# A two-layer mixing, memory and feed-forward block: the queues of four engines ordered by a timeline model

## The chip, the cores and the metric

The kernel runs on one core of a Trainium2 chip. The time is device time in microseconds (us) of one execution; lower is better. The engines are TensorE (PE; PEld is its weight load), VectorE (DVE), ScalarE (ACT), GpSimd (POOL) and SyncE (SP), which issues most loads. Each engine takes its own instructions in order, and waits on semaphores for the others.

## The reference

One sequence of 256 tokens with 2048 columns goes through two layers. Each layer has a mixing step (an RWKV-7 recurrence with 16 heads of 64 beside causal attention with 8 heads on low-rank queries and keys), a cross attention to 256 memory rows, and a feed-forward step of width 8192 with a squared ReLU.

```python
for l in range(DEPTH):
    u = rms_norm(h, mix_pre_g[l])
    proj = u @ w_in[l]                      # layer 1: with w_in_vres beside it
    y_rwkv, v_first = rwkv7_time_mix(proj[..., :RWKV_IN], ...)
    y_mla = mla_heads(proj[..., RWKV_IN:IN_WIDTH], ...)
    y = concatenate([y_rwkv, y_mla]) @ w_out[l]
    h = h + rms_norm(y, mix_post_g[l])
    u = rms_norm(h, mem_pre_g[l])
    h = h + rms_norm(memory_cross_attention(u, mem_n, ...), mem_post_g[l])
    u = rms_norm(h, ffn_pre_g[l])
    y = square(relu(u @ w_ff1[l])) @ w_ff2[l]
    h = h + rms_norm(y, ffn_post_g[l])
```

## The kernel before, in words

Every weight matrix is read once, in units of 512 KB. `units` (L259 on) loads a unit into a buffer `raw` (five of them) from SP. `split` (L283) makes two parts of it: ACT casts `wh` from `raw` (L291), and DVE subtracts to give the rest `wl` (L292). `wh` and `wl` lie in a ring of four buffers, some units in longer-lived ones. The left-hand side has two parts too, and `go` issues three matmuls for each product (`mm`, L243):

```python
    def go(self, o, x, wh, wl, start, stop):
        xh, xl = x
        self.mm(o, xh, wh, start, False)
        self.mm(o, xh, wl, False, False)
        self.mm(o, xl, wh, False, stop)
```

Activations `h` are turned by PE transposes (L248) in blocks of 128 x 512 (`x`). `toT` makes `uf` from such a block on DVE (L397), its first part `uh` on ACT (L398), and the rest `ul` (L399), on DVE for block 0 and on POOL for blocks 1 to 3. `sumsq` (L375) squares `h` on ACT for the norm (tile `junk`); `finish` adds the normed result to `h` on DVE (L455, four rows for each half of the tokens).

In a mixing step the heads come in two groups. `f_group` builds for each group the tiles AR (L658, L663) and BK (L664, L666), products `prod` (L671), and from shifted columns `yp` (L466), `yd` (POOL, L471) the tile vT (L474). In layer 1 vT is mixed with the first layer's values: POOL works on `vf` (L813, L814), DVE adds it (L815). `f_inner` multiplies BK by AR on PE and masks the result to W on DVE (L693); ACT copies pieces to G (L695). `f_fs` then runs 31 steps on DVE, each of a product (L768) and a sum (L770) into T, which give the triangular inverse of a chunk; POOL and ACT copy it to Tb (L775, L776), DVE transposes that to Ud (L779) and Tr (L781), and PE uses Tr with W. Attention has its query copies `qn` on ACT (L1085) and its softmax in `f_lane` (rows L1115 to L1125, maximum `nm` on DVE, exponentials `pr` on ACT). The feed-forward step begins with `ff1_first` (L1320 relu `rf`, L1309 and L1310 its split), then goes on in eight blocks.

The order of PE's queue is written out by hand: fibres (Python generators) are spawned with due times in an estimated time `clk` and polled between matmuls, and this decides where the transposes and small matmuls stand. The scope `tc.manual_schedule(engines={mybir.EngineType.PE})` in `_build` (L1482 on) keeps PE's instructions in the order of the program. The queues of DVE, ACT, POOL and SP are ordered by the framework's own scheduler, from the same program. What it may move is bounded by the data and by buffers: a tile is written only when the readers of its buffer's former content are done.

## Time and profile before

| what | value |
|---|---|
| median of 3 runs (lowest to highest) | 2586.59 us (2586.35 to 2586.64) |
| the profiled execution's own time | 2588.6 us |
| its span, first to last instruction | 2586.8 us |
| mean granted clock of PE | 0.987 |
| PE busy | 2524.0 us (98%) |
| DVE, ACT, POOL busy | 1557.1, 1209.3, 444.6 us |
| data moved by DMA | 456.76 MB, mean 177 GB/s |

The span is what lies between the first and the last instruction of the profiled execution, and 1.8 us less than its own time. In a timeline row the first two numbers are start and duration in us; what stands in brackets at the end is the engine's idle time before the row and what ended it. Names are tiles without their buffer numbers: `g` and `x` are accumulators of PE. In the table of waits the three numbers are the sum, the count and the longest.

### The profile page before, as it was taken

The page shows a single profiled execution, that of the slowest core. Times are in us where ns is not written, and L with a number is a line of the kernel's source. Part 1 is how long each engine was busy: PE and PEld are TensorE (multiplying, and loading weights), DVE is VectorE, ACT ScalarE, POOL GpSimd, SP SyncE. Part 2 cuts the span into 40 slices and gives each one's busy share as a digit, 9 for nine tenths or more (in the row PEclk, how much of TensorE's full clock was granted, in tenths as well). Part 3 has the DMA queues.
Part 4 walks back from the last instruction along what each step waited for, and adds up shares of the span by engine and source line. Part 5 has one row for each costly group of instructions (what it writes and reads, how often), then busy time and mean ns, then how long its engine had stood idle before and what let it go on. Part 6 is the DMA issues. An engine that isn't in the chain of part 4 may idle for free.

```text
span 2586.8 us, 43201 instructions
## 1 busy us (share of the span) xinstructions
PE 2524.0 (98%) x17458; PEld 2285.7 (88%) x17458; DVE 1557.1 (60%) x2121; ACT 1209.3 (47%) x1724; POOL 444.6 (17%) x597
## 2 busy tenths in 40 slices
PE   8999999999999999999999998999999999999998
PEld 7989888989899889989788987889898998899896
DVE  4777966664454555555757778666644555545555
ACT  5454555554444344444454545545544444444443
POOL 3324425220000000000124245202200000000000
PEclk9999999999999999999999999999999999999999
DMA  6454446646656655666654544565456556556663
GB/s 228 151 158 136 132 158 216 216 131 184 191 187 187 188 189 186 188 192 204 199 168 135 158 117 132 168 214 187 136 182 189 187 181 194 190 186 188 192 204 131
DMA packets 257176, 456.76 MB, mean 177 GB/s; under 512 B 25588, under 2 KB 58740, under 8 KB 256976
## 3 DMA queue, kind: packets, MB, share of 16 engines
q1 hardware_dynamic: 247600, 422.79, 51.8%
q0 software_dynamic: 9376, 31.21, 3.8%
q8 instruction: 137, 2.24, 0.4%
q14 instruction: 63, 0.52, 0.1%
HBM read 444.50 MB, written 9.44 MB: 175 GB/s over the span
## 4 chain that ended last, share of the span: by engine, by line
PE 86%; DVE 6%; POOL 2%; issue 2%; DMA 1%; ACT 1%; SPq 0%; DVEq 0%; POOLq 0%; ACTq 0%
PE g L243 77%; PE x L243 7%; DVE wl L292 2%; PE x L248 2%; DVE fs L768 1%; DVE T L770 1%; DVE h L455 1%; DMA raw<-in_w_ff_dram 1%; ACT wh L291 1%; DMA vf<-vfirst 0%; DMA raw<-in_w_in_dram 0%; POOL yd L471 0%; POOL rsn L617 0%; POOL kT L837 0%; POOL vf L814 0%
## 5 line engine op out<-in xcount | busy, mean ns | idle before, releaser
L292 DVE TENSOR_TENSOR wl<-raw,wh 128x1024 fp32r<-128x1024 f32 (+2 forms) x804 | 978.1, 1222 | 736.9 <-ACT wh L291 733.3
L291 ACT CAST wh<-raw 128x1024 fp32r<-128x1024 f32 (+2 forms) x804 | 834.2, 1041 | 980.4 <-PE g L243 903.4
L243 PE MATMUL g<-uh,wh 128*128 128x256 f32 x2816 | 808.1, 287 | 0.0
L243 PE MATMUL g<-uh,wl 128*128 128x256 f32 x2816 | 797.9, 283 | 0.4 <-DVE wl L292 0.4
L243 PE MATMUL g<-ul,wh 128*128 128x256 f32 x2816 | 797.7, 283 | 0.0
L243 PEld LDWEIGHTS g<-uh,wh 128*128 128x128 f32 x2816 | 541.0, 192 | 5.3 <-issue 2.3
L243 PEld LDWEIGHTS g<-uh,wl 128*128 128x128 f32 x2816 | 541.3, 192 | 3.0 <-issue 1.7
L243 PEld LDWEIGHTS g<-ul,wh 128*128 128x128 f32 x2816 | 541.1, 192 | 0.0
L243 PE MATMUL g<-wl,hdh 128*128 128x512 f32 x1024 | 398.9, 390 | 0.4 <-DVE wl L292 0.4
L243 PE MATMUL g<-wh,hdh 128*128 128x512 f32 x1024 | 398.9, 390 | 0.0
L243 PE MATMUL g<-wh,hdl 128*128 128x512 f32 x1024 | 398.5, 389 | 0.0
L1349 POOL TENSOR_TENSOR rl<-rl 128x512 f32<-128x512 f32 x60 | 61.3, 1041 | 1171.6 <-ACT rl L1348 1171.5
L243 PEld LDWEIGHTS g<-wl,hdh 128*128 128x128 f32 x1024 | 192.3, 188 | 40.5 <-DVE wl L292 1.3
L243 PEld LDWEIGHTS g<-wh,hdl 128*128 128x128 f32 x1024 | 192.3, 188 | 39.9
L243 PEld LDWEIGHTS g<-wh,hdh 128*128 128x128 f32 x1024 | 192.3, 188 | 39.4
L243 PE MATMUL g<-wh,uh 128*128 128x256 f32 (+3 forms) x320 | 114.6, 358 | 12.2 <-ACT uh L398 7.9
L243 PE MATMUL g<-wl,uh 128*128 128x256 f32 (+3 forms) x320 | 109.8, 343 | 3.9 <-DVE wl L292 3.9
L243 PE MATMUL g<-wh,ul 128*128 128x256 f32 (+3 forms) x320 | 109.6, 343 | 1.6 <-POOL ul L399 1.1
L1352 DVE TENSOR_TENSOR hdl<-rl,hdh 128x512 fp32r<-128x512 f32 x60 | 47.6, 794 | 67.7 <-ACT hdh L1351 67.7
L1369 DVE SCALAR_TENSOR_TENSOR y<-g,s,y 128x512 f32<-128x512 f32 x112 | 79.0, 744 | 10.6 <-PE g L243 10.6
L243 PEld LDWEIGHTS g<-wh,uh 128*128 128x128 f32 x320 | 63.9, 200 | 19.3 <-ACT uh L398 9.7
L243 PEld LDWEIGHTS g<-wl,uh 128*128 128x128 f32 x320 | 63.9, 200 | 9.6 <-DVE wl L292 5.9
(341 smaller groups left out, 2991.8 us busy)
## 6 DMA issues: line engine op xcount, KB each, us to landing
raw<-in_w_ff_dram SPq DMA_DIRECT2D x512, 512.0 KB, 4.2
raw<-in_w_in_dram SPq DMA_DIRECT2D x112, 512.0 KB, 4.4
raw<-in_w_out_dram SPq DMA_DIRECT2D x64, 512.0 KB, 3.9
raw<-in_wk_mem_dram SPq DMA_DIRECT2D x16, 512.0 KB, 4.1
raw<-in_wq_mem_dram SPq DMA_DIRECT2D x16, 512.0 KB, 3.8
raw<-in_wv_mem_dram SPq DMA_DIRECT2D x16, 512.0 KB, 4.8
raw<-in_wo_mem_dram SPq DMA_DIRECT2D x16, 512.0 KB, 3.6
raw<-in_w_in_dram SPq DMA_DIRECT2D x16, 448.0 KB, 5.1
```

What stands on the lines that cost most here:

```text
L243: return self.nc.tensor.matmul(out, lhsT, rhs, start=start, stop=stop, skip_group_check=skip)
L248: self.nc.tensor.transpose(out, in_, self.ident[p0 : p0 + n, p0 : p0 + n])
L291: nc.scalar.copy(out=wh, in_=raw)
L292: nc.vector.tensor_tensor(out=wl, in0=raw, in1=wh.bitcast(F32), op=ALU.subtract)
L455: nc.vector.scalar_tensor_tensor(out=h[t][c], in0=y[t][c], scalar=rs, in1=h[t][c], op0=ALU.mult, op1=ALU.add)
L768: nc.vector.tensor_tensor(out=tmp, in0=N[:, s + 1 :, s : s + 1].to_broadcast([128, m, w]), in1=T[:, s : s + 1, :w].to_broadcast([128, m, w ...
L770: nc.vector.tensor_tensor(out=T[:, s + 1 :, :w], in0=T[:, s + 1 :, :w], in1=tmp, op=ALU.add)
L1349: nc.gpsimd.tensor_tensor(out=r, in0=r, in1=r, op=ALU.mult)
L1352: nc.vector.tensor_tensor(out=hl[:, 2 * q : 2 * q + 2, :], in0=r, in1=o.bitcast(F32), op=ALU.subtract)
L1369: nc.vector.scalar_tensor_tensor(out=o, in0=ps, scalar=s2[t], in1=o, op0=ALU.mult, op1=ALU.add)
```

## The change

One argument is given to the framework. Its scheduler then plans the order of the queues with its timeline model of the engines; before, it planned without that model.

```diff
-    with tile.TileContext(nc) as tc:
+    with tile.TileContext(nc, schedule_with_timeline_sim=True) as tc:
         _build(nc, tc, aps, out)
```

PE keeps its order, all 15368 rows. DVE has 2041 rows after 2042, and 1551 lines of difference; ACT 738 lines, POOL 240, SP 16, all of these near the program's start: three weight loads and the constants C (L534) now stand ahead of the last four loads of `h`. Nothing is computed in another way, and tiles and buffers are the same. Three places follow, as pieces of the difference: a minus is where a row stood before, a plus where it stands now. The number behind a name tells tiles of the same name apart.

The first piece is DVE's queue in layer 0, at the end of the second group (about 268 to 281 us of the profile before). BK_3021 is written there for the last time, vT_3264 is what PE transposes next, and the `wl` are weight subtractions.

```order
 L664 TENSOR_TENSOR BK_3021<-bb_3224,en_3219 128x4x64
+L466 TENSOR_TENSOR yp_3265<-g_2707,rbc_403 128x2x256
 L665 TENSOR_TENSOR kT_2692<-kT_2692,ka_3226 128x256
-L671 SCALAR_TENSOR_TENSOR prod_3256<-rT_2256,V,kT_2692 128x256
-L666 TENSOR_TENSOR BK_3021<-kT_2692,en_3219 128x4x64
+L466 TENSOR_TENSOR yp_3272<-g_2708,rbc_403 128x2x256
 L671 SCALAR_TENSOR_TENSOR prod_3258<-rT_2256,V,kT_2692 128x256
 L671 SCALAR_TENSOR_TENSOR prod_3260<-rT_2256,V,kT_2692 128x256
+L292 TENSOR_TENSOR wl_3514<-raw_3510,wh_3513 128x1024
+L666 TENSOR_TENSOR BK_3021<-kT_2692,en_3219 128x4x64
```

The last BK row now stands behind the `yp` rows, two more `prod` rows and a `wl`; two further `wl` have moved up, one ahead of this piece and one between the vT rows, all three from places behind the vT and W rows.

The second piece is DVE's queue in layer 1, in the second group (about 1570 to 1582 us). W_16327 is the last of four masked products; vT_16267 is summed with what POOL left in `vf`.

```order
 L693 TENSOR_TENSOR W_16306<-x_16308,C 128x512
-L815 TENSOR_TENSOR vT_16267<-vT_16267,vf_16342 128x512
-L815 TENSOR_TENSOR vT_16267<-vT_16267,vf_16347 128x512
+L292 TENSOR_TENSOR wl_16495<-raw_16491,wh_16494 128x1024
 L693 TENSOR_TENSOR W_16327<-x_16328,C 128x512
 L693 TENSOR_TENSOR W_16327<-x_16329,C 128x512
-L292 TENSOR_TENSOR wl_16495<-raw_16491,wh_16494 128x1024
+L815 TENSOR_TENSOR vT_16267<-vT_16267,vf_16342 128x512
 L700 STREAM_TRANSPOSE N_16358<-G_16224 64x1024
+L815 TENSOR_TENSOR vT_16267<-vT_16267,vf_16347 128x512
```

The two L815 rows, which wait for POOL, have moved behind W, and a `wl` has moved ahead of it.

The third place is the entry of the feed-forward part in layer 1 (about 1846 to 1873 us). On DVE, the rows `uf` of blocks 1 and 2 stand before as follows, and now:

```order
 L451 TENSOR_REDUCE pss_19211<-pp_18990 128x1
+L397 TENSOR_TENSOR uf_19226<-x_19221,V 128x512
+L397 TENSOR_TENSOR uf_19235<-x_19230,V 128x512
 L399 TENSOR_TENSOR ul_18979<-uf_19207,uh_18975 128x4x128
 L455 SCALAR_TENSOR_TENSOR h_16855<-y_18987,prs_19213,h_16855 128x512 x2
 L455 SCALAR_TENSOR_TENSOR h_16856<-y_18988,prs_19213,h_16856 128x512 x2
-L397 TENSOR_TENSOR uf_19226<-x_19221,V 128x512
-L397 TENSOR_TENSOR uf_19235<-x_19230,V 128x512
```

They have moved ahead of the `ul` of block 0 and of the four h rows. On ACT, some 15 us later, wh_19489 is the cast of the last weight unit that `ff1_first` uses for its second quarter:

```order
-L291 CAST wh_19471<-raw_19469 128x1024
 L375 ACTIVATE junk_19441,ss_19440<-h_16855 128x512
 L375 ACTIVATE junk_19443,ss_19440<-h_16855 128x512
 L375 ACTIVATE junk_19445,ss_19440<-h_16856 128x512
 L375 ACTIVATE junk_19447,ss_19440<-h_16856 128x512
-L291 CAST wh_19489<-raw_19487 128x1024
+L291 CAST wh_19471<-raw_19469 128x1024
 L291 CAST wh_19576<-raw_19574 128x1024
-L1320 ACTIVATE rf_19466<-g_19403 128x256
 L291 CAST wh_19582<-raw_19580 128x1024
 L291 CAST wh_19612<-raw_19610 128x1024
+L291 CAST wh_19489<-raw_19487 128x1024
```

The cast wh_19489 stands three casts later, and wh_19471 behind the four `junk` rows; above this piece one `uh` row has moved behind three more `junk` rows. Layer 0 has the same moves at its own entry. Inside the eight feed-forward blocks one `wh` cast has moved ahead of the first split of each half block, and its `wl` likewise.

## The prediction

> **What bounds the kernel now.** I read the page first: busy times, then the chain that ended last.
>
> ```profile
> PE 2524.0 (98%) x17458; PEld 2285.7 (88%) x17458; DVE 1557.1 (60%) x2121; ACT 1209.3 (47%) x1724; POOL 444.6 (17%) x597
> PE 86%; DVE 6%; POOL 2%; issue 2%; DMA 1%; ACT 1%; SPq 0%; DVEq 0%; POOLq 0%; ACTq 0%
> ```
>
> TensorE (PE) is busy for 2524.0 of 2586.8 us, and PE's own queue is the same row for row after the change. So the time can move in two ways only: PE waits more or less, or its matmuls run at another granted clock. Next I read the table of waits of PE, and then the two long feed-forward stretches and two stretches around a wait in the table of stretches (length, busy time of PE, PEld, DVE, ACT, POOL, granted clock, DMA share, GB/s).
>
> ```profile
> PE g L243 <- ACT uh L398: 7.9, 5, 2.0
> PE g L243 <- ACT qn L1085: 6.4, 2, 3.5
> PE x L248 <- DVE vT L474: 5.0, 5, 2.4
> PE g L243 <- DVE wl L292: 4.7, 8, 1.6
> PE g L243 <- ACT wh L291: 4.3, 2, 3.2
> PE x L248 <- DVE rsn L616: 2.1, 2, 1.5
> ...
> 594.00:1258.00 664.00, 664.00 (x4269) 608.46 (x4268) 346.07 (x321) 287.58 (x311) 32.79 (x34) 1.00 0.60 189
> 1884.00:2548.00 664.00, 664.00 (x4270) 608.51 (x4269) 346.02 (x321) 287.66 (x311) 32.78 (x34) 1.00 0.60 189
> ...
> 1846.00:1852.00 6.00, 3.40 (x16) 2.79 (x16) 5.26 (x10) 0.92 (x2) 1.22 (x2) 0.69 0.00 0
> 1852.00:1860.00 8.00, 7.08 (x37) 6.79 (x38) 4.89 (x7) 4.65 (x7) 3.74 (x3) 0.60 0.17 50
> ```
>
> The two feed-forward stretches, 1328 us together, have PE busy for all of their length at clock 1.00: no order of the other queues can gain there. The waits lie in short places of the mixing stages and at the entry of the feed-forward part. Each row has total, count and longest; no wait is longer than 4.3 us, so this is a list of small prices. 0.2% of this kernel is 5.2 us, about what a measurement can tell from no change.
>
> **The change part by part.** No instruction is added. I take the places where PE waits and follow the new queue order by hand, with durations from the rows.
>
> *Start, +1.5 (0 to +4).* SP now issues three weight loads and the constants ahead of the last four loads of `h`, and ACT does two sums of squares (`junk`) ahead of the first `uh` and the second weight cast.
>
> ```profile
> 6.58 3.42 SPq L1402 DMA_DIRECT2D h<-in_x_dram  x4
> 14.15 0.63 ACT L375 ACTIVATE junk<-h 128x512 f32<-128x512 f32 x1
> 13.63 0.74 PE L243 MATMUL g<-wl,uh 128*128 128x448 f32 x1 [1.00 <-DVE wl L292]
> ```
>
> PE already waits there for what follows that cast. Two steps of 0.63 us and their read-outs make 1.5 us; the upper end adds most of the 3.42 us that the four loads are put back.
>
> *State-forming chain of the first group in each layer, −2.6 (−2.6 to +2.3).* The subtractions `wl` (four of 1.22 us) now stand ahead of rows of the serial chain L768/L770. Of the 4.7 us in the `wl` row of the waits, four lie here, one of 1.55 and three of 0.29 to 0.40; these go. The chain's end moves 4 × 1.22 = 4.9 us later, and this is covered:
>
> ```profile
> 157.77 0.41 PE L243 MATMUL g<-wl,uh 128*128 128x320 f32 x1 [1.55 <-DVE wl L292]
> 167.49 0.17 DVE L770 TENSOR_TENSOR T<-T,fs 128x16 f32<-128x16 f32 x1
> 173.95 0.64 POOL L775 COPY Tb<-T 64x512 f32<-64x512 f32 x1
> ```
>
> The next reader of `T` is a copy on POOL, which runs 6.3 us after the chain's end, behind other rows. If that cover were gone, the 4.9 us would count against the 2.6.
>
> *Group steps: first and second group of layer 0, first of layer 1: +1.3 (−4 to +7).* In the second group three `wl` of 1.21 to 1.22 us pass the last BK and vT rows (order shown above).
>
> ```profile
> 269.99 0.41 DVE L666 TENSOR_TENSOR BK<-kT,en 128x256 f32<-128x256 f32 x1
> 275.69 1.21 DVE L292 TENSOR_TENSOR wl<-raw,wh 128x1024 fp32r<-128x1024 f32 x1
> 274.73 1.57 PE L248 MATMUL x<-Id,vT 128*128 128x128 f32 x4 [2.44 <-DVE vT L474]
> ...
> 120.82 0.30 PE L248 MATMUL x<-Id,vT 128*128 128x128 f32 x1 [1.13 <-DVE vT L474]
> 1408.94 1.31 PE L243 MATMUL x<-AR,BK 64*128 64x128 f32 x10 [0.94 <-DVE W L693]
> 1416.19 1.18 PE L243 MATMUL x<-AR,BK 64*128 64x128 f32 x4 [3.92 <-DVE W L693]
> ```
>
> The transposes of vT at 274.73 wait already, so two to three `wl` make them 2.4 to 3.6 us later. But the W rows that follow no longer have these `wl` ahead of them, and reach their old times within 8 us: I take +1.5. The group at 120.82 has the same move with a shorter wait (+1.0). In layer 1 the BK stands about 4 us later (+3.5 at 1403), while W passes one of two L815 rows, which removes most of 0.94 + 3.92 = 4.86: −1.2. Sum +1.3. The lower end keeps only the gains, the upper one only the losses.
>
> *Second group of layer 1, −2.0 (−5 to +2).* Two L815 rows waited for POOL and held W behind them; now `wl` and W stand ahead of both.
>
> ```profile
> 1573.56 1.75 DVE L815 TENSOR_TENSOR vT<-vT,vf 128x512 f32<-128x512 f32 x1 [2.02 <-POOL vf L814]
> 1577.09 1.28 DVE L693 TENSOR_TENSOR W<-x,C 128x512 f32<-128x512 f32 x2
> 1577.83 0.66 PE L248 MATMUL x<-Id,BK 128*128 128x128 f32 x4 [1.72 <-DVE W L693]
> 1582.98 0.39 PE L243 MATMUL g<-qTh,wh 128*128 128x256 f32 x1 [1.07 <-ACT qrx L1061]
> 1585.38 1.12 PE L248 MATMUL x<-Id,vT 128*128 128x128 f32 x4 [0.99 <-ACT tok L722]
> 1627.13 2.12 DVE L781 STREAM_TRANSPOSE Tr<-Tb 64x1024 f32<-64x1024 f32 x1
> 1629.62 1.56 PE L243 MATMUL x<-Tr,W 32*32 32x32 f32 x38
> ```
>
> DVE's idle time began at 1573.56 − 2.02 = 1571.5; W ends at 1571.5 + 1.22 + 1.28 = 1574.0 in place of 1578.4, and 1.72 + 1.07 + 0.99 = 3.8 us of waits go, with about 1 of the 3.5 us for `qn`. But Tr ended 0.37 us before PE wanted it at 1629.62, and the chain before it is all DVE work, with attention rows of about 3 us now put ahead. DVE gets back its idle 2.02 and a little more, less these 3. So most of the 4.8 us is taken back at Tr; I keep 2.0.
>
> *Query copies, layer 0: 0 (−1.4 to +1.5).* The copies `qn` no longer stand behind a softmax row that waits for DVE, which takes 1.4 us from the wait at 319.89; attention rows placed ahead of Tr move its end from 334.97 by 5 to 6 us, to about PE's need.
>
> ```profile
> 319.89 0.80 PE L243 MATMUL g<-wh,oh 128*128 128x512 f32 x1 [2.86 <-ACT qn L1085]
> 332.81 2.16 DVE L781 STREAM_TRANSPOSE Tr<-Tb 64x1024 f32<-64x1024 f32 x1
> 340.74 1.45 PE L243 MATMUL x<-Tr,W 32*32 32x32 f32 x40
> ```
>
> *Entry of the feed-forward part, both layers, −0.4 (−9 to +5).*
>
> ```profile
> 1848.32 2.74 DVE L455 SCALAR_TENSOR_TENSOR h<-y,prs,h 128x512 f32<-128x512 f32 x4 [0.71 <-POOL prs L255]
> 1850.98 1.88 DVE L397 TENSOR_TENSOR uf<-x,V 128x512 f32<-128x512 f32 x3
> 1852.37 0.58 PE L243 MATMUL g<-wh,uh 128*128 128x256 f32 x1 [1.81 <-ACT uh L398]
> 1853.72 0.58 PE L243 MATMUL g<-wh,ul 128*128 128x256 f32 x1 [0.55 <-POOL ul L399]
> 1869.14 1.03 ACT L291 CAST wh<-raw 128x1024 fp32r<-128x1024 f32 x1
> 1872.09 0.28 PE L243 MATMUL g<-wh,uh 128*128 128x256 f32 x1
> ```
>
> Two `uf` now stand ahead of `ul` and the four h rows. 1.81 + 0.55 = 2.4 us of wait go, and `ul` of the first block comes 1.2 us later, where PE waits: −1.2 a layer. Beside that there is the clock: PE's 7.08 busy us at 0.60 would take 4.25 at full clock, so up to 2.8 more; I take half. Against both stands the cast that ends at 1870.2, 1.9 us before PE needs it. It now has all eight `junk` steps and three other casts before it, and its `wl` ends about 2.5 us too late. So 2 × (−1.2 − 1.4 + 2.5) ≈ −0.2, and −0.4 with the slightly longer waits of layer 0.
>
> [...]
>
> *Entry of layer 1 and the group norm, −1.0 (−2 to 0).* In the rows for `wh` (longest 3.2) and `rsn` (2.1 in two) one row each moves ahead by about 0.5 us.
>
> Sum: +1.5 − 2.6 + 1.3 − 2.0 + 0 − 0.4 − 1.0 = −3.2 us. The profiled execution took 2588.6 us with a span of 2586.8, so it would take 2585.4; the median of the runs is 2.0 us lower, 2586.6, and gives **2583.4 us**.
>
> **The rivals.**
>
> A, the gains are kept: DVE has enough idle time that nothing given back is late. −2.6 − 3.8 − 1.4 − 1.0 − 2 × 1.2 − 2 × 1.4 − 1.0 − 0.5 (group steps) + 1.5 = −14.0: 2572.6. For it: DVE is busy for 60%. Against it: at 1627 the chain is DVE's, with 0.37 us to spare.
>
> B, slower: weight subtractions stand ahead of rows that PE waits for. A `wl` row needs its cast on ACT, and DVE stands still behind it. In three group steps the last BK comes 3.4 to 3.5 us late (about 4.8 of push less a margin of 1.4, as at 269.99 against PE's vT at 274.73), 10.2 in all, not regained by W; the casts in front of the feed-forward part cost 5.0 less 2.4; the start 1.5; kept are 2.6 and 2.0: +9.7, 2596.3. It decides as soon as the push of BK is above the margin of 1.4 us and the W rows do not catch up. For it: vT is already waited for in five places. Against it: the same `wl` work leaves later rows free.
>
> C, no effect: the queues differ, but PE's order is fixed and each loss meets a gain of its size: within 1 us, 2586.6. The two stretches without a wait speak for it, the 1577 place against it.
>
> **How the numbers follow.** My forecast 0.44, its own range −9 to +3 (2577.6 to 2589.6); A 0.25; B 0.22; C 0.09. The range takes in A and B with about 2 us beyond each: 2570 to 2598. Faster by over 0.2%: all of A and a third of the forecast, 0.40. Slower: B and a little of the forecast, 0.24. The rest, 0.36, is within 0.2%.
>
> **What would show it.** In the new profile the waits of PE for `wl` around 154 to 167 us should be gone, the `uh` row should fall from 7.9 to about 5, W before 1578 should have no wait, and waits for Tr near 1625 and for `wh` near 1872 should appear. The feed-forward stretches must stay at clock 1.00 with PE fully busy. Wrong would be a wait inside these stretches, a start longer by over 4 us, or PE waits that in sum change by more than 15 us.

## The result and the profile after

The changed kernel is slower: 2600.82 us in the median of four runs (2598.75 to 2602.91), against 2586.57 us (2586.35 to 2586.64) for the kernel before. The ratio is 1.0053, with a 95% interval of 1.004 to 1.0066: 14.2 us more. The forecast was 2583.4 us with a range up to 2598. The profiled execution took 2598.75 us, the lowest of the four, with a span of 2597.0 us and a mean granted clock of 0.988; against the profiled execution of before (span 2586.8) that is +10.2 us, and this is what the traces can account for. The other 4 us are 2.0 by which before's profiled execution lies above its median and 2.1 by which this one lies below its own. What is given below as measured is the median of fast runs, and one execution of 2749.43 us is left out as slow.

The page's busy times and chain of the changed kernel, to be held against the two lines that open the prediction:

```profile
PE 2524.7 (97%) x17458; PEld 2283.2 (88%) x17458; DVE 1576.4 (61%) x2121; ACT 1212.6 (47%) x1724; POOL 457.8 (18%) x597
PE 78%; DVE 7%; ACT 2%; issue 2%; POOL 1%; DMA 1%; DVEq 0%; POOLq 0%; ACTq 0%
```

PE's busy time is the same within 0.7 us, and the rows of the table of waits sum to 59.8 us after and to 49.7 before: over the whole program the 10.2 us appear as waiting. In single places it is otherwise, since the granted clock rose in some (1.00 in place of 0.69 and 0.60 at layer 1's entry) and fell in others (0.79 in place of 1.00 in layer 0's first group). The table of waits of PE, after (sum, count, longest):

```profile
PE g L243 <- DVE wl L292: 8.9, 8, 2.3
PE x L243 <- DVE BK L666: 8.3, 3, 4.1
PE g L243 <- ACT wh L291: 6.5, 5, 3.0
PE x L248 <- DVE vT L474: 5.0, 4, 2.2
...
PE x L248 <- DVE pr L1125: 3.7, 2, 2.4
PE g L243 <- DVE ul L399: 3.4, 4, 1.3
PE x L243 <- DVE ri L1122: 3.3, 1, 3.3
PE x L248 <- POOL qr L1000: 3.1, 1, 3.1
PE g L243 <- ACT uh L398: 2.8, 5, 0.7
```

The waits that the planner was to remove are gone or smaller: `uh` fell from 7.9 to 2.8, `qn` (6.4) and the 4.8 us for W have left the head of the table. In their place stand BK (8.3, no such row before), `pr`, `ri`, `qr`, more `wl` (4.7 before) and more `wh` (4.3 before). So waits were exchanged, at a loss.

Where this happens is seen by taking the same PE instruction in both traces (PE's queue is the same row for row) and subtracting its starts. The table gives how much this distance grew in each part of the program, worked out so from the traces, in us; the last four columns are experiments of the next section.

| part (where it ends in the profile before) | predicted | after | DVE alone planned | DVE alone held | gains only | entries only |
|---|---|---|---|---|---|---|
| start (45) | +1.5 | +3.0 | -0.1 | +1.1 | +0.2 | +0.3 |
| layer 0, first group (137) | +1.0 | +3.8 | +5.5 | +1.6 | 0.0 | 0.0 |
| state-forming chains, both layers | -2.6 | -3.7 | -3.7 | -1.3 | -3.7 | -0.2 |
| layer 0, second group (290) | +1.5 | +3.4 | +5.2 | +2.1 | +0.1 | +0.2 |
| layer 0, `qn` to Tr (345) | 0 | -0.6 | +1.0 | +0.1 | -1.1 | -1.4 |
| entries of the feed-forward part, both, front (556 to 569, 1846 to 1859) | -0.4 with the next row | -12.7 | -10.3 | +0.3 | -10.4 | -10.6 |
| the same, back (to 592, to 1885) | | +13.3 | +6.6 | +3.9 | +4.9 | +4.9 |
| feed-forward, 592 to 1250 and 1885 to 2540 | 0 | 0.0 | 0.0 | 0.0 | 0.0 | 0.0 |
| ends of the feed-forward part (1277, 2575) | not in the sum | +5.2 | -0.5 | +8.0 | +0.2 | +3.3 |
| entry of layer 1 and group norm (1320, 1548) | -1.0 | -2.7 | -2.7 | -1.9 | -3.6 | -1.1 |
| layer 1, first group (1424) | -1.2 | +0.2 | -1.8 | +0.1 | 0.0 | +0.2 |
| layer 1, second group to Tr (1640) | -2.0 | +1.1 | +4.9 | +2.2 | -3.4 | +1.5 |
| sum | -3.2 | +10.3 | +4.1 | +16.3 | -16.7 | -2.9 |

Four places show how these numbers arise, all in the timeline of after. First the second group of layer 0, rows of DVE:

```profile
278.32 1.21 DVE L292 TENSOR_TENSOR wl<-raw,wh 128x1024 fp32r<-128x1024 f32 x1
279.45 0.41 DVE L666 TENSOR_TENSOR BK<-kT,en 128x256 f32<-128x256 f32 x1
...
280.98 1.21 DVE L292 TENSOR_TENSOR wl<-raw,wh 128x1024 fp32r<-128x1024 f32 x1
282.11 0.87 DVE L474 SCALAR_TENSOR_TENSOR vT<-yd,V,yp 128x256 f32<-128x256 f32 x2
```

And the rows of PE that waited there:

```profile
279.92 0.80 PE L243 MATMUL x<-AR,BK 64*128 64x128 f32 x4 [3.96 <-DVE BK L666]
282.64 0.87 PE L248 MATMUL x<-Id,vT 128*128 128x128 f32 x2 [1.06 <-DVE vT L474]
```

This is the first piece of queue that the section on the change shows, in time: the `wl` at 278.32 ends, the last BK row runs, PE starts. Ahead of the wait for vT, which was 2.44 us before and is 1.06 now, there is one of 3.96 us for BK. The same stands in layer 1 at 1416.95, with 4.11 us.

Second, the entry in layer 1, table of stretches after (length, busy time of PE, PEld, DVE, ACT, POOL, granted clock, DMA share, GB/s):

```profile
1846.00:1853.50 7.50, 5.89 (x32) 4.69 (x31) 6.54 (x13) 2.84 (x7) 1.64 (x5) 1.00 0.44 148
1853.50:1862.00 8.50, 6.94 (x55) 6.54 (x56) 8.41 (x10) 3.21 (x6) 4.51 (x4) 1.00 0.00 0
```

And PE's waits in the timeline:

```profile
1852.06 0.39 PE L243 MATMUL g<-wh,uh 128*128 128x256 f32 x1 [0.68 <-ACT uh L398]
1853.87 0.39 PE L243 MATMUL g<-wh,ul 128*128 128x256 f32 x1 [1.30 <-DVE ul L399]
...
1875.25 0.38 PE L243 MATMUL g<-wh,uh 128*128 128x256 f32 x1 [0.98 <-ACT wh L291]
1877.25 0.58 PE L243 MATMUL g<-wl,uh 128*128 128x256 f32 x1 [1.62 <-DVE wl L292]
```

The clock is 1.00 where it was 0.69 and 0.60. The first two of these rows are the same instructions as two rows of before that stand ahead of the waits of 1.81 and 0.55 which the prediction quotes:

```profile
1846.94 0.39 PE L243 MATMUL g<-wh,uh 128*128 128x256 f32 x1 [1.85 <-ACT uh L398]
1847.66 0.39 PE L243 MATMUL g<-wh,ul 128*128 128x256 f32 x1 [0.22 <-DVE ul L399]
```

And this is the table of stretches of before, cut where its clock changed:

```profile
1844.82:1848.24 3.42, 1.35 (x10) 0.90 (x8) 2.77 (x6) 0.62 (x1) 1.17 (x2) 1.00 0.00 0
1848.24:1858.48 10.24, 7.88 (x36) 7.18 (x35) 7.17 (x10) 4.33 (x6) 3.79 (x4) 0.50 0.02 5
```

So the clock fell to 0.50 at 1848.24, behind 1.85 + 0.22 us of waits and ahead of the wait of 1.81, and came back at 1858.48. The front part had 4.4 us of waits before (1.85 + 0.22 + 1.81 + 0.55) and has 2.0 now, since the last two are gone. Of the 6.5 us gained here 2.5 are waits; of the other 4.0 the clock makes most by estimate: 7.88 busy us at 0.50 are 3.9 more than at 1.00 if busy time goes as the clock, and 3.4 by the starts of matmuls of 128x256, which lie 0.21 us apart in this stretch and 0.12 behind 1858.48.

Then comes the other side, waits where before had none: 0.33 for `uh` and 0.86 for `ul` at 1859.82 and 1861.18, then 0.98 for the cast and 1.62 for its subtraction. That is 3.8 us, and the clock is 0.50 from 1877.01 to 1880.42. On ACT the eight sums of squares stand ahead of five casts in a row:

```profile
1869.75 0.62 ACT L375 ACTIVATE junk<-h 128x512 f32<-128x512 f32 x1
1870.27 0.19 ACT L375 ACTIVATION_READ_ACCUMULATOR junk<-h 128x1 f32 x1
1870.36 4.83 ACT L291 CAST wh<-raw 128x1024 fp32r<-128x1024 f32 x5
```

Third, the end of the feed-forward part in layer 1, for which the prediction has no term. Rows of ACT:

```profile
2557.70 2.00 ACT L291 CAST wh<-raw 128x1024 fp32r<-128x1024 f32 x2 [1.69 <-DMA raw<-in_w_ff_dram]
2560.34 2.94 ACT L291 CAST wh<-raw 128x1024 fp32r<-128x1024 f32 x3 [0.64 <-DMA raw<-in_w_ff_dram]
```

And the row of PE:

```profile
2565.39 0.50 PE L243 MATMUL g<-wl,hdh 128*128 128x512 f32 x1 [2.34 <-DVE wl L292]
```

ACT stands still for loads (1.69, 0.64), DVE's subtractions follow it, and on DVE the final sums `y` and `yg` now stand between the last subtractions. PE waits 2.34 us, and the clock is 0.50 from 2566.50 to 2569.91. Before, no wait of ACT there ended with a load, and PE waited 0.21 us.

Fourth, the second group of layer 1, where a gain of 2.0 was forecast. PE's waits:

```profile
1584.68 0.44 PE L248 MATMUL x<-Id,vT 128*128 128x128 f32 x2 [0.44 <-DVE vT L815]
...
1596.44 0.66 PE L248 MATMUL x<-Id,qr 128*128 128x128 f32 x4 [3.15 <-POOL qr L1000]
```

And DVE's rows 35 us later:

```profile
1629.31 1.95 DVE L779 STREAM_TRANSPOSE Ud<-Tb 64x1024 f32<-64x1024 f32 x1
1631.13 1.87 DVE L781 STREAM_TRANSPOSE Tr<-Tb 64x1024 f32<-64x1024 f32 x1
1632.89 0.11 DVE L1122 RECIPROCAL ri<-sum 128x2 f32<-128x2 f32 x1
```

The waits 1.72, 1.07 and 0.99 are gone, one of 0.44 remains, and PE comes 5.2 us earlier to `qr`. There POOL, for which PE waited 0.34 us before, is not ready, and PE waits 3.15. The wait for `qn` is gone too (5.4), and then Tr and the softmax row `ri` behind it take 7.8.

### The profile page after: what moved, and what is told of

Read it like the earlier page. It is cut to its first block, busy times and chain, and to the rows that moved or that the text cites. A ratio compares the mean times of both kernels' runs of the same rounds, so it can differ in the third digit from the quotient of the medians.

```text
span 2597.0 us, 43194 instructions
## 1 busy us (share of the span) xinstructions
PE 2524.7 (97%) x17458; PEld 2283.2 (88%) x17458; DVE 1576.4 (61%) x2121; ACT 1212.6 (47%) x1724; POOL 457.8 (18%) x597
## 4 chain that ended last, share of the span: by engine, by line
PE 78%; DVE 7%; ACT 2%; issue 2%; POOL 1%; DMA 1%; DVEq 0%; POOLq 0%; ACTq 0%
PE g L243 71%; PE x L243 6%; DVE wl L292 2%; PE x L248 1%; ACT wh L291 1%; DVE h L455 1%; DMA raw<-in_w_ff_dram 1%; DVE uf L397 0%; ACT junk L375 0%; POOL rsn L617 0%; DVE x L1115 0%; DVE fs L768 0%; DVE T L770 0%; ACT pr L1120 0%; DVE prod L671 0%
## 5 line engine op out<-in xcount | busy, mean ns | idle before, releaser
L292 DVE TENSOR_TENSOR wl<-raw,wh 128x1024 fp32r<-128x1024 f32 (+2 forms) x804 | 993.3, 1239 | 817.9 <-ACT wh L291 816.8
L1369 DVE SCALAR_TENSOR_TENSOR y<-g,s,y 128x512 f32<-128x512 f32 x112 | 79.0, 743 | 13.3 <-PE g L243 13.2
L243 PEld LDWEIGHTS g<-wh,ul 128*128 128x128 f32 x320 | 64.0, 200 | 12.2 <-DVE ul L399 4.6
```

Source lines behind the costliest of these rows:

```text
L243: return self.nc.tensor.matmul(out, lhsT, rhs, start=start, stop=stop, skip_group_check=skip)
L292: nc.vector.tensor_tensor(out=wl, in0=raw, in1=wh.bitcast(F32), op=ALU.subtract)
L1369: nc.vector.scalar_tensor_tensor(out=o, in0=ps, scalar=s2[t], in1=o, op0=ALU.mult, op1=ALU.add)
```

## The experiments

All experiments hold parts of the queues in the order of the kernel before and let the planner decide the rest. This is done by order edges between instructions of one engine, which add no wait on a semaphore and take away none of the data's. The numbers are instructions of the program, and each list is a piece of one engine's queue before. Four kernels ran on each of three chips beside the kernel before, whose medians there were 2587.47 (the first four), 2588.28 (the next four) and 2587.70 us (the last four).

**DVE alone planned.** ACT, POOL and SP keep their order of before over the whole program.

```diff
+class _TC(tile.TileContext):
+    log = []
+
+    def instruction_hook(self, instruction):
+        self.log.append(instruction)
+        super().instruction_hook(instruction)
...
+def _chain(tc, chains):
+    by = {i.name: i for i in tc.log}
+    info = mybir.DependencyInfo(mybir.DependencyClass.NoSync, mybir.DependencyReason.DATA)
+    for c in chains:
+        c = [n for n in map("I-{}".format, c) if n in by]
+        for a, b in zip(c, c[1:]):
+            tc.add_manual_dep(by[b], a, info, reason="queue order")
...
-    with tile.TileContext(nc, schedule_with_timeline_sim=True) as tc:
+    with _TC(nc, schedule_with_timeline_sim=True) as tc:
```

> Here only DVE's queue is planned with the timeline model; ACT, POOL and SP are held in their order of before. Theory (local places): the 14 us are the sum of about ten places where a weight cast or a weight subtraction now stands ahead of rows that PE waits for, less the gains elsewhere. The losses at the entry of the feed-forward part and at its end begin with casts on ACT, so they go (about 10 and 5 us), while the gains on DVE stay: 2580 to 2590. Rival 1 (DVE alone does it): as the changed kernel, 2598 to 2603. Rival 2 (no place counts, the changed kernel is slower all over or by its clock): no clear change from 2600 either.

Measured: 2593.92 us, ratio 1.0023 (1.0014 to 1.0033), about 4 us above the theory's range and clearly below rival 1. The group steps together and the second group of layer 1 lose more than after (table above), so DVE's own order is enough for these losses. The ends of the feed-forward part lose nothing, but the back part of the entries still loses 6.6.

**DVE alone held.** The opposite: DVE keeps its order, the others are planned.

```diff
+        [53, 120, 129, 138, 122, 147, 155, 161, 167, 173, 212, 434, 224, 245, 234, 266, 236, 255, 287, 276, 297, 345, 437, 380, 386, 445, 495, 416,
...
```

> The other half: DVE's queue is held in its order of before, ACT, POOL and SP are planned with the timeline model. Theory (local places): the start (+3) and the casts put late at the feed-forward entry (+5 in each layer) stay, the late BK rows of the groups go, and so do the gains of DVE: 2592 to 2602. Rival 1 (DVE alone does it): about 2587. Rival 2 (slower all over): about 2600.

Measured: 2604.75 us, ratio 1.0063 (1.0048 to 1.0078), slower than the change itself and than either theory allowed. The entries gain nothing (+0.3 in place of -12.7), the ends of the feed-forward part lose 8.0, and the group steps 3.8 of the 7.4 in after: the new order of the other engines without DVE's gives mostly costs. At the end of layer 0 PE waits 2.67 us for a `wl`.
**Single places put back.** Four kernels each hold one kind of place in the order of before, on all four engines, and leave the rest as after: the two ends of the feed-forward part; the back part of its two entries; the three group steps; the first 45 us. Of the first, two of its eight lists:

```diff
+        [12961, 12962, 16845],
...
+        [25658, 25699, 25711, 25723, 25735, 25753, 25765, 25777, 25789, 25885, 25886, 25887, 25888],
```

> The changed kernel, with the order of before put back at one place in each layer: the last block of the feed-forward part (1240 to 1277 and 2530 to 2575 us of the profile before), on all four engines. Theory (local places): the waits of PE for wl of 1.64 and 2.34 us there go, and with them 1.5 and 3.8 us of drift: 5.3 us less than the changed kernel, 2595 to 2596. Rival 2 (the time only moves to the next wait, or is lost all over): less than 1.5 us.

Measured: 2593.09 us, 1.0019 (1.001 to 1.0029).

> The changed kernel, with the order of before put back in each layer from 564.5 to 592 us and from 1855 to 1884 us of the profile before: the casts and sums of squares in front of the feed-forward part, not the uf rows ahead of them. Theory (local places): the waits of PE for wh (0.95, 0.98) and wl (1.64, 1.62) there go with the slower clock behind them: 8 to 12 us less than the changed kernel, 2589 to 2593. Rival 2: less than 2 us. Rival 3 (the uf rows are the cost, by the ul they put back): 1 to 4 us.

Measured: 2594.02 us, 1.0023 (1.0013 to 1.0032).

> The changed kernel, with the order of before put back at the three group steps (105 to 136, 262 to 290 and 1390 to 1421 us of the profile before). Theory (late BK and vT behind weight subtractions): the drifts of +3.8 and +3.2 us in layer 0 go, in layer 1 the +0.2 becomes about 0: 6 to 7 us less than the changed kernel, 2593 to 2595. Rival (the groups are bound by all the work of DVE, so the order there only says which wait comes last): less than 2 us.

Measured: 2594.33 us, the median of five runs from 2586.23 to 2597.91, 1.0023 (1.0007 to 1.0039).

> The changed kernel, with the order of before put back in the first 45 us, the loads on SP among it. Theory: the +3.0 us of drift at the start go, nothing else moves: 2597 to 2598.5. Rival (the first weights are bound by their loads in either order): within 1 us of the changed kernel.

Measured: 2592.59 us, 1.0018 (1.0009 to 1.0028).

Each of the four is 6 to 8 us below after's 2600.82, 29 us in sum; with all four sorts put back at once (below) it is 20. Only the group steps came out where their theory put them; the ends and the start gave more, the entries a little less. So the parts do not add. In the first, layer 1's end went from +3.7 to 0.0 as expected, but layer 0's end only from +1.4 to +1.2, and the back part of the entries, whose order was not touched, also came out 4.6 us better in its profiled execution. So the single numbers cannot be read as prices.

One reason is in the trace of the third. In layer 0's first group PE's waits for vT are again those of before within 0.2 us in sum, and yet 1.2 us are lost there, with the clock at 0.50 for 3.41 us:

```profile
125.20:128.61 3.41, 3.12 (x8) 2.33 (x9) 3.41 (x10) 1.16 (x2) 2.45 (x8) 0.50 0.41 154
```

Before, the clock was 1.00 behind nearly the same waits; the last section sets the two beside each other. The next question was whether the changed kernel itself varies so much.

**The changed kernel again**, with the helper but no list.

```diff
+def _chains():
+    return [
+    ]
```

> The changed kernel once more, beside the others of this call on the same chip, since single places put back gave more than their ledger share (7.7 and 8.2 us less in place of 5.3 and 3.0). Theory (the changed kernel's time depends on the chip and the run, because casts wait for loads): below 2600, about 2596 to 2599, with a spread of some us. Rival (the places are not independent, and undoing one frees more than its own): 2600 to 2602 as before.

Measured: 2599.87 us, 1.0047 (1.003 to 1.0063), its runs from 2594.04 to 2600.73. The result stands, between what the two theories say, but one run in four came 5 us below the other three. That one is the profiled execution. Its trace has the same order and ends 4.8 us earlier, 2.7 of it at layer 1's end. There ACT's last casts, which start when their loads land, come 0.8 us earlier against PE than in the first trace, PE waits 1.24 us in place of 2.34, and the clock stays at 1.00: matmuls of 128x512 start 0.23 us apart on both sides of the wait. The rows of ACT and PE in its timeline:

```profile
2557.49 2.98 ACT L291 CAST wh<-raw 128x1024 fp32r<-128x1024 f32 x3 [0.93 <-DMA raw<-in_w_ff_dram]
...
2562.26 0.50 PE L243 MATMUL g<-wl,hdh 128*128 128x512 f32 x1 [1.24 <-DVE wl L292]
```

So a part of after's loss hangs on when loads land, and a single trace gives such a place within some 3 us only. Whether loads are behind all of the 5 us is open.

**Gains only.** Before's order everywhere but in seven stretches, those where the table shows a gain (139 to 172, 292 to 324, 540 to 564.5, 1424 to 1457, 1500 to 1592, 1598 to 1618, 1832 to 1855 us of before). One of its 31 lists:

```diff
+        [16746, 16613, 16817, 16625],
...
```

> The order of before everywhere but in seven stretches where PE gained in the changed kernel (139 to 172, 292 to 324, 540 to 564.5, 1424 to 1457, 1500 to 1592, 1598 to 1618, 1832 to 1855 us of the profile before); there the framework plans with the timeline model. Theory (local places that add up): gains of 3 (first chain), 3.7 (norm of layer 1) and 2.5 to 3 in each feed-forward entry stay, those at the second group of layer 1 are given back at Tr: 10 to 13 us less than before, 2574 to 2577. Rival (each gain is given back at the next place that DVE or ACT bounds): within 4 us of before.

Measured: 2572.78 us (2572.04 to 2575.2), 0.9944 (0.9928 to 0.996): faster than both kernels, and by 15.5 us on its chip where the theory said 10 to 13. Its page shows how, in the line of busy times:

```profile
PE 2511.4 (98%) x17458; PEld 2274.6 (89%) x17458; DVE 1566.9 (61%) x2121; ACT 1210.8 (47%) x1724; POOL 450.3 (18%) x597
```

Its waits sum to 46.1 us, only 3.6 less than the 49.7 of before. The first rows of its table of waits are old ones (vT, W) and one that has come in (`ml`):

```profile
PE x L248 <- DVE vT L474: 5.1, 5, 2.5
PE x L243 <- DVE W L693: 4.9, 2, 3.9
...
PE x L243 <- DVE ml L1139: 4.2, 2, 2.3
```

The gain is in PE's busy time, 2511.4 in place of 2524.0, 12.6 us: the same matmuls at a mean clock of 0.993 in place of 0.987. Between its first rise and PE's last matmul the clock was at 0.50 for 61.4 us before and for 27.3 us here (54.6 in after). What the good moves save is mostly clock.

**Fewer gains.** As the last, but the second group of layer 1 and its attention are held as well.

```diff
-        [16414, 16519, 16639, 16521, 16522, 16524, 16525, 16527, 16528, 16596, 16597, 16599, 16600, 16602, 16740],
-        [16746, 16613, 16817, 16625],
-        [16402, 16886, 16888, 16890],
...
```

> As the one with seven stretches, but the second group of layer 1 and its attention (1546 to 1618 us) are in the order of before too. Theory (local places): the same within 2 us if what is gained there is given back at Tr, 2574 to 2578. Rival (the second group's 5 us are kept): 4 to 6 us slower than the kernel with seven stretches.

Measured: 2576.93 us, 0.9959 (0.9944 to 0.9974), 4.15 more than the last, as the rival said. That group keeps a gain as long as the attention rows and Tr behind it stay in the old order: -4.8 + 1.5 - 5.0 + 5.0 = -3.3 in the traces, where the whole change has +1.1.

**Losses back.** From the other side: the changed kernel with before's order at all places where it lost, the four sorts above together.

```diff
+        [53, 120, 129, 138, 122, 147, 155, 161, 167, 173, 212, 434, 224, 245, 234, 266, 236, 255, 287, 276, 297, 345, 437, 380, 386, 445, 495, 416,
...
+        [12961, 12962, 16845],
...
```

> The changed kernel, with the order of before put back at all eight loss places at once: the start, three group steps, the back part of both feed-forward entries and the ends of both feed-forward parts. Theory (local places, ledger of the traces): left are -3.1, -0.6 and -3.7 on the gain side, about -2.7 in each entry and -0.6 and +1 around attention: 11 us less than before, 2574 to 2578. Rival (losses are all over, not only there): no faster than before.

Measured: 2580.57 us, 0.9975 (0.9966 to 0.9985), 20.3 below after by the two medians, but 2.6 above the theory's range, its runs from 2577.39 to 2588.11. It still has the losses around `qr` and Tr in layer 1.

**Entries only.** Before's order everywhere but in the first part of the two entries, where `uf` moves ahead.

```diff
+        [51, 34252, 121, 130, 204, 139, 154, 148, 160, 166, 206, 172, 208, 210, 223, 244, 265, 235, 286, 256, 277, 303, 298, 337, 339, 341, 343, 379,
...
```

> The order of before everywhere but at the feed-forward entries (540 to 564.5 and 1832 to 1855 us), where the uf rows stand ahead as in the changed kernel. Theory (the 6 us gained there are partly given back in the next 20 us, whatever else is changed): 2 x 2.7 = 5.4 us less than before, 2581 to 2583. Rival A (the gain is kept when the casts behind it stand as before): 10 to 12 us less. Rival B (it is given back in full): within 1.5 us of before.

Measured: 2583.31 us, 0.9981 (0.9972 to 0.999), 4.4 below before on its chip where the theory said 5.4. In its trace, of the slowest of its runs (2585.78), the entries gain 6.3 and 4.3 us and give back 3.1 and 1.9 within 25 us, although the order there is that of before: PE, now earlier, waits for `uh` and `ul` in layer 0 and for a `wl` in both layers. It also has 3.3 us at the end of layer 0, where its order is before's too. There ACT waited for a load, and PE behind it:

```profile
1255.64 3.90 ACT L291 CAST wh<-raw 128x1024 fp32r<-128x1024 f32 x4 [2.21 <-DMA raw<-in_w_ff_dram]
...
1263.93 0.50 PE L243 MATMUL g<-wl,hdh 128*128 128x512 f32 x1 [1.88 <-DVE wl L292]
```

**Sums late.** Gains only, and beside it the eight sums of squares (`junk`) at each entry moved behind the casts that PE waits for there. The DVE and ACT lists from there on begin so in layer 0:

```diff
-        [6417, 6492, 6419, 6444, 6533, 6471, 6485, 6502, 6518, 6550, 6622, 6598, 6640, 6727, 6616, 6733, 6763, 6655, 6667, 6798, 6693, 6717, 6828,
+        [6417, 6492, 6419, 6444, 6533, 6471, 6485, 6502, 6550, 6622, 6640, 6727, 6616, 6733, 6763, 6655, 6667, 6798, 6693, 6717, 6518, 6598, 6828,
...
-        [6418, 6532, 6445, 6484, 6472, 6510, 6503, 6512, 6514, 6516, 6549, 6621, 6590, 6592, 6594, 6596, 6639, 6726, 6615, 6732, 6762, 6797, 6654,
+        [6418, 6532, 6445, 6484, 6472, 6503, 6549, 6621, 6639, 6726, 6615, 6732, 6762, 6797, 6654, 6666, 6692, 6716, 6510, 6512, 6514, 6516, 6590,
...
```

> The one with seven stretches, and in the back part of the feed-forward entries the sums of squares (eight junk rows, with the small rows that end them) moved behind all other rows of that place on ACT, DVE and POOL. Theory (ACT's queue of uh, junk and casts is what takes part of the gain back there): 2 to 4 us faster than the kernel with seven stretches, 2569 to 2571. Rival (the chain of uf, uh and ul for the second half of the tokens takes it back, not the sums): within 1 us of it.

Measured: 2570.61 us (2567.71 to 2572.97), 0.9932 (0.9917 to 0.9947), the lowest of all and within the theory. Its lead over gains only is not clear of the noise: the two ran on different chips and the intervals of their ratios overlap. In the traces the back part of the entries loses 2.4 us in place of 4.9. At layer 1's entry PE has no wait left in the back part; in ACT's timeline the casts come as two runs of three ahead of the `junk` rows:

```profile
1847.59 2.94 ACT L291 CAST wh<-raw 128x1024 fp32r<-128x1024 f32 x3
1852.80 2.94 ACT L291 CAST wh<-raw 128x1024 fp32r<-128x1024 f32 x3
...
1866.38 0.64 ACT L375 ACTIVATE junk<-h 128x512 f32<-128x512 f32 x1
```

## Why the prediction was wrong, point by point

The forecast was -3.2 us against +10.2 in the profiled executions: 13.4 us apart. The places were mostly named rightly, the costs of the group steps were taken too small, and one place was left out. These are the two steps that failed. Of the two, the group steps are the surer: in the second trace of the changed kernel they lose 6.7 us, and the ends 2.6.

- **Ends of the feed-forward part: the step that is missing, +5.2.** The prediction looked at 594 to 1258 and 1884 to 2548, found PE full, and went from "no order of the other queues can gain there" to a sum without any term for this part. The stretches did stay full (0.0 in every kernel). But the part goes on for some 25 us behind each, where in after ACT's casts wait for the loads of the last units (rows above). For layer 1 the cause is shown to be ACT's new order, since POOL has no row there and SP's order differs only near the start: six kernels with before's order there lose 0.0 to 0.1 us, and the one with DVE alone planned gains 0.5; after and five others with ACT planned lose 1.0 to 4.0. For layer 0 it is not settled: ACT planned loses 1.4 to 4.1, ACT as before 0.0 to 3.3, the 3.3 behind the late load shown above.
- **Group steps: +1.3 foreseen, +7.4 measured.** The mechanism was named (`wl` ahead of BK and vT), and rival B even had its size for the two groups of layer 0, 3.4 to 3.5 us each (3.8 and 3.4 measured); in layer 1 a wait of 4.11 us for BK came and those of 0.94 and 3.92 for W went, +0.2. What failed is "reach their old times within 8 us: I take +1.5". PE has no wait for W there, but it has waited 3.96 us at 279.92 by then, and up to 290 it has not made this good. In layer 0's first group the difference in waits alone is small. PE's waits for vT in the timeline of after:

```profile
124.87 0.30 PE L248 MATMUL x<-Id,vT 128*128 128x128 f32 x1 [2.17 <-DVE vT L474]
125.64 0.33 PE L248 MATMUL x<-Id,vT 128*128 128x128 f32 x1 [0.47 <-DVE vT L474]
127.25 0.87 PE L248 MATMUL x<-Id,vT 128*128 128x128 f32 x2 [1.27 <-DVE vT L474]
```

And, beside the 1.13 that the prediction quotes, before:

```profile
121.91 0.33 PE L248 MATMUL x<-Id,vT 128*128 128x128 f32 x1 [0.79 <-DVE vT L474]
122.65 0.33 PE L248 MATMUL x<-Id,vT 128*128 128x128 f32 x1 [0.41 <-DVE vT L474]
123.18 0.33 PE L248 MATMUL x<-Id,vT 128*128 128x128 f32 x1 [0.21 <-DVE vT L474]
```

The stretch in after's table of stretches:

```profile
125.00:141.00 16.00, 14.25 (x96) 10.69 (x95) 11.76 (x21) 6.95 (x10) 3.93 (x10) 0.79 0.26 75
```

And the same stretch in the table of before:

```profile
121.00:137.00 16.00, 14.59 (x108) 11.10 (x108) 14.53 (x24) 8.54 (x13) 3.87 (x10) 1.00 0.33 97
```

  Before, there were waits of 1.13, 0.79, 0.41 and 0.21, 2.5 us in all; after, 3.9. That is 1.4 us more of waiting, and the place lost 3.8: the rest fits the clock, 0.79 in place of 1.00. It was 0.50 from 125.97 to 132.79, where PE was busy for 5.55 us, an estimated 2.4 to 2.8 more than at 1.00, worked out as for the entry in layer 1. The prediction put the clock into the entries and forgot it here.
- **Second group of layer 1: -2.0 foreseen, +1.1 measured.** That the gain is taken back at Tr was right, 7.8 us of it. Not seen was POOL's `qr`, 3.15 us: the prediction followed DVE's chain and took POOL, 17% busy, for free.
- **Entries: -0.4 foreseen, +0.5 measured.** The net is right by luck, since both halves were two and a half times too small: per layer 2.6 us gained and 2.5 lost were foreseen, 6.2 and 6.5 gained and 6.6 and 6.7 lost were measured. The gain was too small because half of 2.8 us was taken for the clock, where an estimated 3.4 to 3.9 went with it. It was also counted only from 1852.00 on, about where the wait of 1.81 ends: the clock had fallen at 1848.24, behind 1.85 + 0.22 = 2.07 us of waits. Of the loss, the order of casts and sums is about half: with the order of before put back there (the second of the single places) each layer still loses 3.4 us, which the prediction has no term for.
- **Start: +1.5 foreseen, +3.0 measured**, within its bounds. It lies in the order of ACT, POOL and SP: with these held it is -0.1. Which of the two causes named, the sums of squares or the later loads of `h`, is not separated. Only 0.6 us of it is waiting; beside that the clock is on record at 1.00 from 23.57 us in place of 18.69, and matmuls of 128x448 start 0.37 us apart ahead of these points and 0.21 behind them.
- **State-forming chains -2.6 (-3.7), `qn` of layer 0: 0 (-0.6), entry of layer 1 and norm -1.0 (-2.7).** Right in sign, the last by luck. In the norm half a microsecond was foreseen for a wait for `rsn`; PE still waits at the same row, 1.38 us for `oc` in place of 1.46 for `rsn`, and all waits there are only 0.4 us less, while the stretch gave 3.7. The table of stretches before:

```profile
1520.00:1550.00 30.00, 26.95 (x235) 24.13 (x234) 22.19 (x47) 16.32 (x39) 19.43 (x28) 0.89 0.39 108
```

And after:

```profile
1528.00:1555.00 27.00, 24.39 (x240) 22.40 (x240) 23.26 (x45) 15.82 (x39) 20.81 (x28) 1.00 0.47 123
```

  The clock rose from 0.89 to 1.00, and that is what the sum had no term for.

These differences sum to the 13.4 us: 5.2 + 6.1 + 3.1 + 0.9 + 1.5 - 1.1 - 0.6 - 1.7 = 13.4. Rival B came nearest: it had the mechanism of the larger part, slower by weight subtractions ahead of rows that PE waits for, and its 2596.3 us is 4.5 us below the median. That its +9.7 is so near the +10.2 of the traces is in part luck, since it has no term for the ends either and takes 3.5 us for a group in layer 1 that lost 0.2.

Of what was named beforehand: the `wl` waits of the first group's chain are gone and `uh` fell (to 2.8, not 5), as forecast; a wait near 1872 for `wh` appeared, at 1875.25. The wait for W at 1577.83 is gone, and at Tr's matmuls there is one of 3.27 us, which ended with `ri`. "PE waits that in sum change by more than 15 us" did not happen (+10.1), and the start is not longer by over 4.

## What to carry to other kernels

When an engine that is nearly always busy sets the time, every place where its suppliers are only just in time is a price that a new order can raise, and gains elsewhere can run into the next supplier: cost the losses at each place with the clock in them, and do not let a later catch-up cancel a wait of the bounding engine. A planned queue can be better taken by stretches than as a whole: here the same planner costs 14.2 us over the program and gains some 15 where its order is kept only at seven places. Look at the last microseconds of a long steady part apart from the part itself, since here a full steady stretch said nothing about its end.

## What the runs showed of the hardware

In the traces of before and after the granted clock of PE is on record from 18.69 and 23.57 us on, as 1.00 or 0.50, and up to PE's last matmul it changes only at points that lie whole multiples of 3.41 us apart: before, it was 0.50 from 1848.24 to 1858.48, three such steps, and in after from 125.97 to 132.79, two. Cut at these points, the two traces have 17 steps at clock 1.00 in which PE stood idle for 1.88 us or more by the profile's busy times, and each was followed by 0.50. Of 5 steps with 1.44 to 1.88 us idle one was, and of 1442 with less one, with 1.43. In some of the steps followed by 0.50 two shorter waits stand in place of a long one: before, PE was idle for 0.98 and 0.99 us between 1582.00 and 1585.41, and in after for 0.95 and 1.13 between 583.35 and 586.77, while one wait of 1.72 between 1575.17 and 1578.59 of before was followed by 1.00. The waits for vT in layer 0's first group show what the borders can do: before, a border at 121.09 parts the 1.13 us from the 1.41 behind it, and the clock stays at 1.00; with the group steps put back nearly the same waits (1.15, 0.79 and a part of the next) fall into one step, from 121.78 to 125.20, and the clock is 0.50 from there to 128.61. That it is the sum of the waits within one step which counts fits these cases, but it is read from them and was not tried by a run. The borders lie differently in each trace: the record of 1.00 begins at 18.69 us before, at 23.57 in after and at 21.48 in the second trace of the same kernel. How much of the scatter between runs this makes is not shown.

So a table of waits alone understated a wait and its removal here. Layer 0's first group waited 1.4 us more and lost 3.8, and the kernel with the gains only has 3.6 us less of waits than before and 12.6 us less busy time of PE. Over the whole change the two agree (10.1 us of waits, 10.2 of time), because the clock gained at the entries and lost elsewhere. And with the same order of every queue the time of the changed kernel went from 2594.04 to 2600.73 us on one chip.
